# Attention mixers written as planned jobs, pinned in order, with tiles laid out in whole lines

## The chip, the cores and the metric
One core of one Trainium2 chip. The metric is device time in microseconds (us). Three runs of the kernel before gave 1289.66, 1289.69 and 1290.18 us, so the median is 1289.69 us.

## The reference, cut to what matters
Two layers over 512 tokens of width 1024, in float32. Each layer is a mixer and then a gated MLP, each behind an RMSNorm and added to the residual; a last RMSNorm ends it.

```python
def reference(x, ...):
    for layer in range(2):
        h = rmsnorm(x, attn_norm[layer])
        if layer % 2 == 0:   # 8 stick-breaking heads + 8 native-sparse heads, one w_in, one w_out
            x = x + even_mixer(h, ...)
        else:                # 16 forgetting-attention heads, softmax(q k^T * scale + cum_q - cum_k), causal
            x = x + odd_mixer(h, ...)
        x = x + conv_glu_ffn(rmsnorm(x, ffn_norm[layer]), ...)
    return rmsnorm(x, final_norm)
```
A stick-breaking head weighs key s by sigmoid(z) times the product of (1 - sigmoid(z)) over later keys, so it needs a reversed cumulative sum along the keys. A native-sparse head adds three gated branches: 31 compressed blocks, selected blocks and a window. With 512 tokens the selection takes every block and the window every key, so both of those are plain causal softmax.

## The kernel before, in words
The activations are kept transposed: eight tiles of 128 features by 512 tokens. Float32 products are made of three fp32r products: a part is split in a high half (ACT, a cast, line 193) and a low half (DVE, a subtraction, line 194), and high x high, low x high and high x low are added in PSUM. One **step** is these three matmuls for one 128-row slice; a **unit** is the eight steps that give 128 output features (line 197). `vgroup` makes values for 128 tokens at a time, `proj` (line 473) multiplies attention outputs by the output weights and adds to the residual. Weight parts are loaded by SP into two `wraw` buffers and split into two `whi`/`wlo` buffers.

Attention runs in pairs of heads, four stick-breaking pairs (`SbPair`) and eight native-sparse ones in layer 0, eight forgetting ones in layer 1. A pair is: scores S on PE, for query blocks 3, 2 and then 0 and 1; for softmax pairs a masked add with a running maximum on DVE (line 401) and the exponential on ACT (line 403), for stick-breaking pairs three ACT functions, scans on DVE and one more ACT function; for softmax pairs a scaling by the inverse sum on POOL (line 416, four instructions for two query blocks); five groups T of four transposes on PE, each copied to the tile `ph` by ACT (lines 425, 426); and the products V with the values. There is one PSUM bank for T, one for V, two double banks for S, two for the dense steps.

`pipeline` walks over the pairs and lays S of one pair, T of the pair before and V of the pair before that in one sequence, and after each piece takes a number of dense steps from the list `Fill`: 28 steps over a pair in the stick-breaking part and 6 later in layer 0, 22 in layer 1. The instructions of each engine then stand in a fixed order. The part of `proj` that uses the first four output tiles is among the fillers; the part with the last four comes after the last pair.

Small tiles (sums, maxima, gates, tables) lie between the large ones in the same pools, and the value parts are 264 or 272 columns wide, so the large tiles behind them begin at different places in a 256-byte line: counting their sizes, `XH` and `XL` begin 32 bytes into one, the output tiles `OH`, `OL` 192 (layer 0) or 160 bytes (layer 1).

Of the kernel before, what the change touches and what calls it, by code (L numbers as in the profile page):

```python
# [70 lines left out]
def pipeline(pairs, fill, steps):  # L71

    p1 = p2 = None
    for n, h in enumerate(list(pairs) + [None, None]):
        seq = []
        if h is not None:
            seq.append(lambda: (h.S((3,)), h.S((2,))))
        if p2 is not None:
            seq.append(p2.V)
        if p1 is not None:  # L80
            seq.append(lambda: p1.T(0))
        if h is not None:
            seq.append(lambda: h.N(2))
        if p1 is not None:
            seq.append(lambda: p1.T(1))
        if h is not None:
            seq.append(lambda: h.S((0, 1)))
        if p1 is not None:
            seq.append(lambda: p1.T(2))
        if h is not None:  # L90
            seq.append(lambda: h.N(0))
        if p1 is not None:
            seq += [lambda: p1.T(3), lambda: p1.T(4)]
        f = steps(n)
        done = 0
        for m, a in enumerate(seq):
            a()
            want = f * (m + 1) // len(seq)
            fill.step(want - done)
            done = want  # L100
        p2, p1 = p1, h
# [3 lines left out]
def trunk(ctx, tc, A):  # L105
    nc = tc.nc
    pe, act, dve, pool, sp = nc.tensor, nc.scalar, nc.vector, nc.gpsimd, nc.sync
# [49 lines left out]
    maskb = cp.tile([P, 2, 2, P], BF, name="maskb")  # L157
# [5 lines left out]
    def load_consts():  # L163
        for t, n in ((ones, "ones"), (ident, "ident"), (mask32, "mask2"), (mk, "mk"), (conv, "conv")):
            sp.dma_start(t, A[n])
        pool.tensor_copy(maskb, mask32)

    def warm():

        z = cp.tile([P, SEQ], BF, name="zero")  # L170
        pool.memset(z, 0.0)
        ps = pp.tile([P, SEQ], F32, tag="t", bufs=1, name="t")
        for n in range(12):
            mm(ps, z[:, 0:P], z, n == 0, n == 11)


    def weights(src, shape, alloc=None, pieces=1):

        w = wp.tile(shape, F32, tag="wraw", bufs=2, name="wraw")
        if pieces > 1:  # L180
            h = wp.tile(shape, F32R, tag="whi", bufs=2, name="whi")
            l = wp.tile(shape, F32R, tag="wlo", bufs=2, name="wlo")
# [5 lines left out]
        if alloc is not None:  # L188
            h, l = alloc(shape)
        else:  # L190
            h = wp.tile(shape, F32R, tag="whi", bufs=2, name="whi")
            l = wp.tile(shape, F32R, tag="wlo", bufs=2, name="wlo")
        act.copy(h, w)  # L193
        dve.tensor_sub(l, w, h.bitcast(F32))  # L194
        return h, l
# [70 lines left out]
    def finish(fp, src, oh, ol):  # L266
# [20 lines left out]
        def square(m, b, ps):  # L287
# [3 lines left out]
            sq = wp.tile([P, SEQ], F32, tag="sq2", bufs=4, name="sq")  # L291
# [64 lines left out]
    HALF = (slice(0, 64), slice(64, 128))  # L356

    class Pair:

        def __init__(self, ap, q, k, vt, vh, get_o, first, last, bias=None, gate=None, extra=None, done=None):
            self.__dict__.update(locals())
            self.started = False

        def start(self):
            if self.started:
                return
            self.started = True
            self.q, self.k = self.q(), self.k()  # L370
            if self.bias is not None:
                self.bias = self.bias()
            self.e = self.ap.tile([P, 2, 1280], F32, tag="e", bufs=2, name="e")
            self.nm = self.ap.tile([P, 2, NB], F32, tag="nm", bufs=2, name="nm")
            self.dn = self.ap.tile([P, 2, NB], F32, tag="dn", bufs=2, name="dn")

        def scores(self, ii, more):

            self.start()
            ps = s_banks()  # L380
            for i in ii:
                w = P * (i + 1)
                o = EOFF[i] - EOFF[ii[0]]
                t = slice(i * P, i * P + P)
                for hd, r in enumerate(HALF):
                    mm(ps[:, hd, o:o + w], self.q[r, t], self.k[r, 0:w], True, more is None)
                if more is not None:
                    for hd, r in enumerate(HALF):
                        more(ps[:, hd, o:o + w], r, i)
            return ps  # L390

        def S(self, ii):
            ps = self.scores(ii, None)
            for i in reversed(ii):
                w = P * (i + 1)
                o = EOFF[i] - EOFF[ii[0]]
                for hd in range(2):
                    ei = self.e[:, hd, EOFF[i]:EOFF[i] + w]
                    nm, dn = self.nm[:, hd, i:i + 1], self.dn[:, hd, i:i + 1]
                    add = mk[:, 384 - P * i:512] if self.bias is None else self.bias[:, hd, EOFF[i]:EOFF[i] + w]  # L400
                    dve.tensor_tensor_reduce(ei, ps[:, hd, o:o + w], add, scale=-1.0, scalar=3.0e38,  # L401
                                             op0=ALU.add, op1=ALU.min, accum_out=nm)
                    act.activation(ei, ei, AF.Exp, bias=nm, scale=-1.0, accum_out=dn)  # L403
            if self.extra is not None and 0 in ii:
                self.extra.S()

        def N(self, b):

            dn = self.dn[:, :, b:b + 2]
            dve.reciprocal(dn, dn)  # L410
            if self.gate is not None:
                dve.tensor_mul(dn, dn, self.gate[:, :, b:b + 2])
            for i in (b + 1, b):
                for hd in range(2):
                    ei = self.e[:, hd, EOFF[i]:EOFF[i] + P * (i + 1)]
                    pool.tensor_scalar(ei, ei, self.dn[:, hd, i:i + 1], 1.0, op0=ALU.mult, op1=ALU.mult)  # L416

        def T(self, n):
            if n == 0:
                self.ph = self.ap.tile([P, 2560], F32, tag="ph", bufs=1, name="ph")  # L420
            ps = pp.tile([P, SEQ], F32, tag="t", bufs=1, name="t")
            for hd, j in TGRP[n]:
                for i in range(j, NB):
                    o = POFF[hd][j] - 512 * n + (i - j) * P
                    pe.transpose(ps[:, o:o + P], self.e[:, hd, EOFF[i] + j * P:EOFF[i] + j * P + P], ident)  # L425
            act.copy(self.ph[:, 512 * n:512 * n + 512], ps)  # L426
            if self.extra is not None and n == 4:
                self.extra.T()

        def V(self):  # L430
            vt, o = self.vt(), self.get_o()
            for j in (0, 1, 3, 2):
                w = SEQ - j * P
                for hd, r in enumerate(HALF):
                    p0 = POFF[hd][j]
                    mm(o[r, j * P:SEQ], vt[:, self.vh + hd, j], self.ph[:, p0:p0 + w],
                       self.first and j == 0, self.last and j == 2)
            if self.done is not None:
                self.done(o)

    class SbPair(Pair):


        def S(self, ii):
            def more(ps, r, i):
                for n in range(2):
                    mm(ps[:, i * P:i * P + P], maskb[r, 0, n], maskb[r, 1, n], False, n == 1)
            ps = self.scores(ii, more)
            e0 = EOFF[ii[0]]
            w = sum(P * (i + 1) for i in ii)  # L450
            z, e = ps[:, :, 0:w], self.e[:, :, e0:e0 + w]
            lt = self.ap.tile([P, 2, SEQ], F32, tag="lt", bufs=2, name="lt")
            l = lt[:, :, 0:w]
            act.activation(l, z, AF.Abs)  # L454
            act.activation(l, l, AF.Exp, scale=-1.0)
            act.activation(l, l, AF.Ln, bias=1.0)
            dve.scalar_tensor_tensor(l, z, 0.0, l, op0=ALU.max, op1=ALU.add)  # L457
            for i in ii:
                o = EOFF[i] - e0
                for hd in range(2):  # L460
                    ei, li = e[:, hd, o:o + P * (i + 1)], l[:, hd, o:o + P * (i + 1)]
                    dve.tensor_tensor_scan(ei[:, ::-1], li[:, ::-1], li[:, ::-1], 0.0, op0=ALU.add, op1=ALU.bypass)  # L462
            dve.tensor_sub(e, z, e)  # L463
            act.activation(e, e, AF.Exp)
# [578 lines left out]
```

## Time and profile before
| | us |
|---|---|
| median of the runs | 1289.69 |
| the profiled execution, its own time | 1291.93 |
| its span, first to last instruction | 1290.1 |
| PE busy, DVE busy, ACT busy, POOL busy | 1271.2, 693.7, 555.7, 147.9 |
| layer 0: head and first units; attention; last part of the output projection | 0 to 41; 41 to 292; 292 to 313 |
| MLP 0 | 313 to 674 |
| layer 1: norm and first units; attention; last part of the output projection | 674 to 726; 726 to 899; 899 to 921 |
| MLP 1 and the final norm | 921 to 1290 |

Busy time of PE counts a matmul from its start to a modelled end, so two matmuls in a row overlap, and a short wait can hide in it. Where PE's own pace matters, the starts of its instructions are compared.

### The profile page before, as it was taken

Reading aid. Unit: us, or ns where it says so; the run is one execution under the profiler, and the core shown is the slowest. Engines: PE = TensorE matmul, PEld = TensorE weight load, DVE = VectorE, ACT = ScalarE, POOL = GpSimd, SP = SyncE. Lnnn points to the kernel's source line nnn. Section 1 sums busy time; section 2 is a strip of 40 time slices with the busy share of each in tenths; the row PEclk is TensorE's granted clock in tenths of the full one; section 3 lists DMA queues with packets and bytes.
Section 4 is the critical chain, followed back from the end, with each engine's and each line's share of the span. In section 5 each row is a group of like instructions: output and inputs, shape, how many; then the busy total and the mean of one; then the engine's idle time right before and its main releaser. Section 6 shows DMA issues by size and latency. Waiting matters only on the chain.

```text
span 1290.1 us, 16521 instructions
## 1 busy us (share of the span) xinstructions
PE 1271.2 (99%) x6338; PEld 1002.1 (78%) x6338; DVE 693.7 (54%) x1142; ACT 555.7 (43%) x948; POOL 147.9 (11%) x206
## 2 busy tenths in 40 slices
PE   8999999999999999999999999999999999999997
PEld 5876856567888888888888877866788888888886
DVE  7468665538655434565443443344755543556534
ACT  6556465645433223334342554444533322333442
POOL 0000042223000000000111433321200000000010
PEclk9999999999999999999999999999999999999999
DMA  6315201003333233232344453411333223333232
GB/s 224 95 59 147 87 21 42 19 26 123 98 99 94 78 106 107 92 98 89 94 127 141 145 151 92 120 51 51 122 98 98 88 90 100 108 94 94 88 99 90
DMA packets 50639, 124.00 MB, mean 96 GB/s; under 512 B 6320, under 2 KB 15792, under 8 KB 50560
## 3 DMA queue, kind: packets, MB, share of 16 engines
q1 hardware_dynamic: 49040, 121.35, 31.0%
q10 hardware_dynamic: 1520, 1.59, 0.4%
q8 instruction: 50, 0.82, 0.3%
q14 instruction: 29, 0.24, 0.1%
HBM read 119.28 MB, written 2.13 MB: 94 GB/s over the span
## 4 chain that ended last, share of the span: by engine, by line
PE 93%; DVE 3%; ACT 2%; issue 1%; DMA 1%; SPq 0%; DVEq 0%; ACTq 0%
PE mm L115 80%; PE s L115 6%; PE o L115 4%; PE t L425 3%; DVE e L462 1%; DVE wlo L194 0%; ACT whi L193 0%; DMA x<-x 0%; ACT xh L248 0%; DMA wraw<-wu 0%; DVE lt L457 0%; DVE acc L239 0%; ACT lt L454 0%; DVE e L463 0%; DVE e L401 0%
## 5 line engine op out<-in xcount | busy, mean ns | idle before, releaser
L115 PE MATMUL mm<-xh,whi 128*128 128x512 f32 x936 | 372.2, 398 | 0.9 <-ACT xh L248 0.6
L115 PE MATMUL mm<-xh,wlo 128*128 128x512 f32 x936 | 365.1, 390 | 1.6 <-DVE wlo L194 1.6
L115 PE MATMUL mm<-xl,whi 128*128 128x512 f32 x936 | 365.5, 391 | 0.1
L193 ACT CAST whi<-wraw 128x1024 fp32r<-128x1024 f32 (+2 forms) x219 | 200.0, 914 | 383.5 <-PE mm L115 362.7
L194 DVE TENSOR_TENSOR wlo<-wraw,whi 128x1024 fp32r<-128x1024 f32 (+2 forms) x219 | 236.4, 1079 | 137.4 <-ACT whi L193 134.7
L115 PEld LDWEIGHTS mm<-xh,whi 128*128 128x128 f32 x936 | 175.8, 188 | 44.8 <-issue 8.8
L115 PEld LDWEIGHTS mm<-xl,whi 128*128 128x128 f32 x936 | 175.8, 188 | 40.0 <-DVE xl L249 1.8
L115 PEld LDWEIGHTS mm<-xh,wlo 128*128 128x128 f32 x936 | 176.1, 188 | 37.0 <-DVE wlo L194 2.2
L115 PE MATMUL mm<-gh,whi 128*128 128x512 f32 (+2 forms) x352 | 135.0, 383 | 0.0
L115 PE MATMUL mm<-gl,whi 128*128 128x512 f32 (+2 forms) x352 | 134.8, 383 | 0.0
L115 PE MATMUL mm<-gh,wlo 128*128 128x512 f32 (+2 forms) x352 | 134.8, 383 | 0.0
L416 POOL TENSOR_SCALAR e<-e,dn 128x512 f32<-128x512 f32 (+3 forms) x128 | 78.1, 629 | 176.9 <-DVE dn L410 83.9
L403 ACT ACTIVATE e<-e,nm 128x512 f32<-128x512 f32 (+3 forms) x128 | 70.4, 551 | 50.2 <-DVE nm L401 50.2
L426 ACT COPY ph<-t 128x512 f32<-128x512 f32 x100 | 58.1, 581 | 69.6 <-PE t L425 69.4
L783 DVE TENSOR_TENSOR a<-mm,rstd 128x512 f32<-128x512 f32 x44 | 30.4, 691 | 92.1 <-PE mm L115 91.9
L237 POOL COPY acc<-sq 128x512 f32<-128x512 f32 x4 | 2.8, 706 | 651.4 <-ACT sq L234 651.4
L489 DVE TENSOR_TENSOR x<-x,mm 128x512 f32<-128x512 f32 x62 | 42.6, 686 | 64.2 <-PE mm L115 63.9
L115 PEld LDWEIGHTS mm<-gh,wlo 128*128 128x128 f32 x352 | 66.1, 188 | 13.0
L115 PEld LDWEIGHTS mm<-gl,whi 128*128 128x128 f32 x352 | 66.1, 188 | 12.8
L115 PEld LDWEIGHTS mm<-gh,whi 128*128 128x128 f32 x352 | 66.1, 188 | 12.8
L791 DVE TENSOR_TENSOR b<-mm,rstd 128x512 f32<-128x512 f32 x44 | 30.4, 692 | 72.4 <-PE mm L115 72.3
L787 ACT ACTIVATE tt<-tt 128x512 f32<-128x512 f32 x44 | 27.8, 632 | 86.8 <-DVE tt L786 86.8
(167 smaller groups left out, 1644.3 us busy)
## 6 DMA issues: line engine op xcount, KB each, us to landing
wraw<-wfi SPq DMA_DIRECT2D x88, 512.0 KB
wraw<-wu SPq DMA_DIRECT2D x31, 512.0 KB
wraw<-wfo SPq DMA_DIRECT2D x32, 384.0 KB
wraw<-wfo SPq DMA_DIRECT2D x32, 320.0 KB
wraw<-wo SPq DMA_DIRECT2D x32, 256.0 KB
cb<-cd SPq DMA_DIRECT2D x8, 512.0 KB
x<-x SPq DMA_DIRECT2D x14, 256.0 KB
wraw<-wv SPq DMA_DIRECT2D x6, 528.0 KB
```

Source lines behind the costliest of these rows:

```text
L115: pe.matmul(out, l, r, start=st, stop=sp_)
L193: act.copy(h, w)
L194: dve.tensor_sub(l, w, h.bitcast(F32))
L403: act.activation(ei, ei, AF.Exp, bias=nm, scale=-1.0, accum_out=dn)
L416: pool.tensor_scalar(ei, ei, self.dn[:, hd, i:i + 1], 1.0, op0=ALU.mult, op1=ALU.mult)
L425: pe.transpose(ps[:, o:o + P], self.e[:, hd, EOFF[i] + j * P:EOFF[i] + j * P + P], ident)
L426: act.copy(self.ph[:, 512 * n:512 * n + 512], ps)
L462: dve.tensor_tensor_scan(ei[:, ::-1], li[:, ::-1], li[:, ::-1], 0.0, op0=ALU.add, op1=ALU.bypass)
L489: dve.tensor_add(X[m], X[m], ps)
L783: dve.tensor_mul(a, ps, rstd)
L787: silu.append(act.activation(t, t, AF.Silu).ins)
L791: dve.tensor_mul(b, ps, rstd)
```

## The change
Both mixers are no longer walked over by `pipeline`. Every piece becomes a `Job` of one engine with a cost in microseconds, the jobs that it needs, a priority, and tokens for the buffers that it takes and gives back. `Plan.run` is a list scheduler inside the kernel: it goes forward in planned time, picks on each engine the job that can begin first (among those within 0.03 us the one with the smallest priority number), and calls it. While it runs, every instruction of PE, ACT, DVE, POOL and SP is pinned in the order in which it was called. Priorities on PE are V 10, T 20, S 30 and dense steps 100 and up; elsewhere weight loads and splits have 1.2, output copies 1, the work on scores 2. The cost of a job is written out by hand.

Also: `ph` gets two buffers (one before); the first values of layer 0 move from the part ahead of the attention into the plan; the gates' 24 columns, spread before over three value groups (3 x 264), go to the last (256, 256, 280); output projections load two or four tiles' weights as one part, and for output tiles 4 to 7 the two late slices that are ready earlier are multiplied ahead of the last pair (four more adds to the residual on DVE in each layer); rows of `whi` and `wlo` are rounded up to whole multiples of 128 bytes, small tiles go to a pool of their own at the end, `maskb` and `zero` leave the first pool. The rope needs one buffer less. The MLPs and the final norm are unchanged. After it, every tile that a dense matmul reads begins 32 bytes into a line, by the sizes.

```diff
-def pipeline(pairs, fill, steps):
...
+class Plan:
+    LAG = 0.08
...
+    def _when(self, j):
+        t = self.free[j.eng]
+        for d in j.deps:
+            if d.end is None:
+                return None
+            if d.eng != j.eng:
+                t = max(t, d.end + (0.25 if d.eng == "PE" else self.LAG))
+            elif d.lat:
+                t = max(t, d.end + self.LAG)
+        for n in j.take:
+            if not self.bufs[n]:
+                return None
+            t = max(t, min(self.bufs[n]) + self.LAG)
+        return t
+
+    def run(self):
+        while self.jobs:
...
+            for r in ready.values():
+                t0 = min(t for t, _ in r)
+                t, j = min((x for x in r if x[0] <= t0 + self.wait.get(x[1].eng, 0.03)), key=lambda x: x[1].prio)
+                if best is None or t < best[0]:
+                    best = t, j
...
+            self.free[j.eng] = t + j.cost
+            j.end = t + j.cost + j.lat
...
+            j.fn()
...
+    def weight_parts(shape):
+        wide = [P, shape[1], -(-shape[2] // 32) * 32]
+        return [wp.tile(wide, F32R, tag=t, bufs=2, name=t)[:, :, 0:shape[2]] for t in ("whi", "wlo")]
...
+        def weights(self, src, shape, place=None, token="w", split=None):
...
+            a = self.plan.add("SP", 0.35, load, self.prev_load, prio=p, take=("wraw",), lat=3.3)
+            b = self.plan.add("ACT", 0.19 + 0.00085 * n, hi, a, prio=p, take=(token,))
+            c = self.plan.add("DVE", 0.16 + 0.00104 * n, lambda: dve.tensor_sub(...), b, prio=p, give=("wraw",))
...
+        def dense(self, w, k0, n, mv, after=(), end=True):
...
+                j = self.plan.add("PE", 0.69, step, w[1], j, *(after if k == 0 else ()), prio=100 + self.seq, ...)
...
+                j = plan.add("PE", 0.1 + 0.00167 * w2 + (0.1 if sb else 0), S, q[1], k[1], ..., prio=30 + u + 0.001 * len(sj),
+                             take=("s", "e") if ii == (3,) else ("s",), give=give if ii == (0, 1) else ())
...
+                        ex[i, hd] = plan.add("POOL", 0.28 + 0.0008 * P * (i + 1), sc, j, prio=2 + u)
...
+                j = plan.add("PE", 0.42, T, *need, tj[0] if tj else None, prio=20 + u + 0.001 * g,
+                             take=("t", "ph") if g == 0 else ("t",), give=())
+                tj.append(plan.add("ACT", 0.6, lambda g=g: act.copy(...), j, prio=1, give=("t",)))
...
+            j = plan.add("PE", 2.4 + (0.64 if cmp else 0), V, vt[1], self.prev_v, *need, ..., prio=10 + u, ...)
...
-            pipeline(pairs, fl, lambda n: 28 if n < 4 else 6)
-            fl.add(*[proj(m, [(A["wo0"][m][:, 4:8], 4)], OH[4:], OL[4:], lambda m: feed(m, 1)) for m in range(NK)])
+            part([6, 7], 0, 4, (oj[6],))
+            part(range(4, 8), 4, 2, (oj[6],))
+            part([0, 1], 4, 4, (oj[7],), last)
+            part([2, 3], 4, 4, (oj[7],), last)
+            part(range(4, 8), 6, 2, (oj[7],), last)
+            inorder[0] = True
+            plan.run()
```

## Rows read from the trace of the kernel before

**Rows 1.** The page's first part: the span, and for each engine its busy time, share of the span and instructions.
```profile
span 1290.1 us, 16521 instructions
PE 1271.2 (99%) x6338; PEld 1002.1 (78%) x6338; DVE 693.7 (54%) x1142; ACT 555.7 (43%) x948; POOL 147.9 (11%) x206
```

**Rows 2.** Busy time of each engine in stretches: the stretch, its length, then PE, weight loads (PEld), DVE, ACT and POOL, each with its count, then the granted clock, the share of the DMA engines and GB/s.
```profile
41.00:165.00 124.00, 120.35 (x792) 95.71 (x792) 81.81 (x115) 72.06 (x109) 1.61 (x4) 0.99 0.30 91
165.00:292.00 127.00, 125.16 (x670) 75.66 (x668) 70.52 (x226) 73.07 (x192) 38.03 (x66) 1.00 0.09 27
313.30:673.60 360.30, 360.17 (x1587) 297.62 (x1586) 190.37 (x237) 129.59 (x163) 10.35 (x8) 1.00 0.31 97
726.00:884.00 158.00, 158.00 (x935) 120.53 (x934) 65.72 (x171) 77.36 (x186) 54.40 (x80) 1.00 0.37 102
884.00:899.40 15.40, 15.15 (x79) 8.68 (x77) 4.12 (x7) 6.03 (x11) 0.00 (x0) 1.00 0.10 29
920.80:1267.00 346.20, 346.07 (x1538) 286.70 (x1536) 181.72 (x225) 124.36 (x157) 7.14 (x6) 1.00 0.31 95
```

**Rows 3.** The chain that ended last, in order of time: start, length, engine, tile, line and count. The first two are dense stretches, the last part of layer 0's output projection with the start of the MLP, and the MLP; then a scores block, a run of two dense steps and a V block of layer 1.
```profile
292.05 21.42 PE mm L115 x92
320.60 348.46 PE mm L115 x1536
...
746.36 1.70 PE s L115 x8
748.06 1.58 PE mm L115 x6
749.64 2.30 PE o L115 x16
```

**Rows 4.** PE's instructions in order of time at six places in layer 0 and, last, at one in layer 1 where a run of dense steps begins behind a scores block: start, length, line, operation, out<-in, shapes, count, and in brackets the idle time before and what ended it.
```profile
82.73 0.50 PE L115 MATMUL mm<-xh,whi 128*128 128x512 f32 x1
83.63 0.50 PE L115 MATMUL mm<-xh,wlo 128*128 128x512 f32 x1 [0.40 <-DVE wlo L194]
...
92.45 0.39 PE L115 MATMUL mm<-xl,whi 128*128 128x512 f32 x1
94.05 0.66 PE L425 MATMUL t<-ident,e 128*128 128x128 f32 x4 [1.21 <-ACT ph L426]
...
125.37 0.87 PE L115 MATMUL s<-k,q 64*128 64x384 f32 x4
128.28 0.85 PE L115 MATMUL mm<-wc,gt 128*62 128x64 f32 x10 [2.04 <-DVE wlo L194]
...
252.88 0.66 PE L425 MATMUL t<-ident,e 128*128 128x128 f32 x4
253.82 0.71 PE L115 MATMUL s<-k,q 64*128 64x128 f32 x6 [0.29 <-DVE nm L401]
...
286.15 2.37 PE L115 MATMUL o<-ph,vt 128*64 128x512 f32 x14
289.19 0.50 PE L115 MATMUL mm<-o,whi 128*128 128x512 f32 x1 [0.68 <-ACT o L470]
...
290.22 0.63 PE L115 MATMUL mm<-o,whi 128*128 128x512 f32 x2
291.49 0.46 PE L115 MATMUL mm<-o,whi 128*128 128x512 f32 x1 [0.63 <-DVE x L489]
292.05 0.50 PE L115 MATMUL mm<-o,wlo 128*128 128x512 f32 x1
...
747.99 0.50 PE L115 MATMUL mm<-xh,whi 128*128 128x512 f32 x1
748.33 0.40 PE L115 MATMUL mm<-xh,wlo 128*128 128x512 f32 x1
```

**Rows 5.** Groups of instructions by line, engine, operation and shape, over the whole run: count, then busy time in us, mean ns of one, and idle time before them with what ended it. The splits of a whole part on ACT and DVE and the copy of a transposed group on ACT.
```profile
L194 DVE TENSOR_TENSOR wlo<-wraw,whi 128x1024 fp32r<-128x1024 f32 x122 | 151.1, 1239 | 53.5 <-ACT whi L193 53.4
...
L193 ACT CAST whi<-wraw 128x1024 fp32r<-128x1024 f32 x122 | 128.4, 1052 | 216.1 <-PE mm L115 198.5 <-DMA wraw<-wu 11.8 <-PE s L115 4.0
L426 ACT COPY ph<-t 128x512 f32<-128x512 f32 x100 | 58.1, 581 | 69.6 <-PE t L425 69.4
```

**Rows 6.** The same view for POOL's scalings, and for PE's weight loads of T and V.
```profile
L416 POOL TENSOR_SCALAR e<-e,dn 128x512 f32<-128x512 f32 x32 | 23.9, 759 | 102.9 <-DVE dn L410 30.4 <-DVE dn L412 24.4 <-ACT oh L470 21.8
L416 POOL TENSOR_SCALAR e<-e,dn 128x384 f32<-128x384 f32 x32 | 21.9, 696 | 0.0
L416 POOL TENSOR_SCALAR e<-e,dn 128x128 f32<-128x128 f32 x32 | 17.0, 542 | 0.0
L416 POOL TENSOR_SCALAR e<-e,dn 128x256 f32<-128x256 f32 x32 | 16.1, 517 | 74.0 <-DVE dn L410 53.5 <-ACT ph L426 18.5 <-DVE dn L412 2.0
...
L425 PEld LDWEIGHTS t<-ident,e 128*128 128x128 f32 x400 | 46.2, 140 | 24.2 <-ACT ph L426 9.2 <-issue 4.8 <-POOL e L416 2.7
L115 PEld LDWEIGHTS o<-ph,vt 128*64 128x64 f32 x320 | 21.6, 136 | 24.2 <-issue 23.0 <-ACT ph L426 0.5 <-DVE nm L401 0.2
```

**Rows 7.** Instructions in order of time in layer 1: four scalings on POOL in one pair, the DVE split that ran beside them, and the same four scalings in the next pair.
```profile
762.90 2.59 POOL L416 TENSOR_SCALAR e<-e,dn 128x256 f32<-128x256 f32 x4 [5.33 <-DVE dn L410]
...
763.57 1.34 DVE L194 TENSOR_TENSOR wlo<-wraw,whi 128x1024 fp32r<-128x1024 f32 x1 [0.76 <-ACT whi L193]
...
786.03 1.63 POOL L416 TENSOR_SCALAR e<-e,dn 128x256 f32<-128x256 f32 x4 [8.96 <-DVE dn L410]
```

More of the change, by code (lines that the diff above doesn't have):

```diff
@@ L68, in get, with __init__, __getattr__, call @@
         return d[key]
-def pipeline(pairs, fill, steps):
[L73 to L101, printed above, removed]
+class Ordered:
+    def __init__(self, tc, engine, on, dma=False):
+        self.tc, self.engine, self.on, self.dma = tc, engine, on, dma
+    def __getattr__(self, name):
+        f = getattr(self.engine, name)
+        if name.startswith("preload") or (name.startswith("dma") and not self.dma):
+            return f
+        def call(*a, **k):
+            r = f(*a, **k)
+            if self.on[0]:
+                self.tc.keep_in_program_order(r)
+            return r
+        return call
@@ L187, in weights @@
         sp.dma_start(w, src)
[L188 to L192, printed above, removed]
         act.copy(h, w)
@@ L356, in trunk @@
     HALF = (slice(0, 64), slice(64, 128))
[L358 to L387, printed above, removed]
-                    for hd, r in enumerate(HALF):
[L389 to L464, printed above, removed]
-        def N(self, b):
-            pass
@@ L543, in k_use, with v_use @@
                 return use
-            def v_use(key, j):
+            def v_use(key):
                 def use(tb, ps):
@@ new lines, in values, with out, gate_rows @@
+            def values(key, g, n, places=((v_own, "vw"), (None, "w")), more=None):
+                tag = "vn" if key == "n" else "vt" + "AB"[key]
+                def out(tb):
+                    if tb == 0:
+                        VT[key] = ap.tile([P, 4, NB, 64], F32, tag=tag, bufs=1, name="vt")
+                    return VT[key]
+                a = A[f"wv0_{g}"]
+                return M.values([a[0], a[1]], n, places, out, more)
+            def gate_rows(tb, b, j):
+                return plan.add("ACT", 0.26, lambda: act.activation(gates[:, tb], b["ps"][:, 256:280], AF.Exp, scale=nrt[:, tb:tb + 1]),
+                                j, prio=1, give=("mm",))
@@ new lines, in layer0 @@
+            for p in range(4):
+                oj[p] = M.pair(p, *SB[p], (lambda p=p: VT[p // 2], v1 if p > 1 else v0), 2 * (p % 2), lambda p=p: o_tiles(p),
+                               sb=True, give=("q", "k"))
+            part = lambda ms, a, n, after, use=None: M.project(A["wo0"], ms, a, n, OH, OL, after, use)
+            for kind, p in order:
+                if kind == "q":
+                    nq[p] = NQ(p)
+                else:
+                    part([p, p + 1], 0, 4, (oj[3], lx))
@@ new lines, in layer0 @@
+            for p in range(4):
+                c = dict(p=p, bd=ck, vz=cvz, cm=cm, cv=cv, gate=gate, gj=gj)
+                o = {}
+                for b, key in ((1, ks), (2, kw)):
+                    oj[4 + p] = M.pair(4 + 2 * p + b - 1, nq[p], key, (lambda: VT["n"], vn), 2 * (b - 1), (lambda p=p: o_tiles(4 + p)) if b == 2 else None,
+                                       gate=gate[:, b, 2 * p:2 * p + 2], gj=gj, cmp=c if b == 1 else None, o=o, first=False, last=b == 2,
+                                       give=("q",) if b == 2 else ())
@@ new lines, in layer1 @@
+            part = lambda ms, a, n, after, use=None: M.project(A["wo1"], ms, a, n, OH, OL, after, use)
+            oj = {}
+            for p in range(NK):
+                oj[p] = M.pair(p, *R[p], (lambda p=p: VT[p // 2], vj[p // 2]), 2 * (p % 2), lambda p=p: o_tiles(p), bias=gates(p),
+                               give=("q", "k"))
+                if p % 2:
+                    plan.add("SP", 0.0, lambda: None, M.prev_v, prio=0, give=("vt",))
+            for m in range(0, NK, 2):
+                part([m, m + 1], 0, 4, (oj[3],))
@@ L941, in trunk @@
+            part(range(4, 8), 4, 2, (oj[5],))
+            last = lambda m, j: M.feed(m, 3, j)
+            part([0, 1], 4, 4, (oj[7],), last)
+            part([2, 3], 4, 4, (oj[7],), last)
+            part(range(4, 8), 6, 2, (oj[7],), last)
+            inorder[0] = True
+            plan.run()
+            inorder[0] = False
     layer1()
```

671 lines of the change are left out of this document (481 added, 190 removed).

## The prediction, made before the change was run
> **What bounds the kernel now.** The page's first part comes first: PE is busy 99% of the span, DVE 54% and ACT 43% [rows 1]. By itself that says little, since a matmul's end is modelled. So the stretches come next [rows 2]: the reader is to see that PE has no idle time at all over the main part of layer 1's attention (158.00 us of 158.00), almost none in the MLPs, and 3.65 + 1.84 us in layer 0's attention; and that no other engine is full there (DVE 66% at most). Then the chain, for PE's own pace [rows 3]: in the MLP 1536 matmuls of 512 columns take 348.46 us, 226.9 ns each; in the last part of layer 0's output projection 92 take 21.42 us, 232.8 ns each. Last the order of time on PE around its waits, by starts [rows 4]. The kernel is bound by PE's work. What an order of jobs can give back is the time in which PE waits, not the work.
>
> **What the change removes: PE's waits.** Neighbouring starts in layer 0, less what the same neighbours need when nothing is late [rows 4]. A first matmul after a scores block: 0.90 us, where layer 1 shows 0.34, so 0.56. Last step before a transpose: 1.60 less 0.23 is 1.37. Scores before the compression products: the 2.04 that stand in brackets. Transposes before a block of scores: the 0.29 in brackets. V (14 matmuls, 3.03 us) less the 2.30 of a whole block [rows 3]: 0.73. The first projection step behind the last pair: 1.27 less 0.46, and 0.56 less 0.23, together 1.14. The sum is 6.1 us. Each has a cause that an order with more filler can cover: a weight split that comes late, a copy, an ACT output copy after the last pair. Layer 1 has no idle time to give back before 884 us, and 0.25 us after [rows 2]; I count nothing there. So the removal is worth 6.1 us if nothing takes the place of these waits, and zero if the new order only moves them.
>
> **What it adds: new waits from a tight order.** The list scheduler puts V, T and S ahead of dense steps as soon as its costs say that they can begin. Once pinned, PE stands still when such a job is late, with ready dense steps behind it. So I hold the written costs against the rows. A dense step costs 0.69; three matmuls at 226.9 ns are 0.681 [rows 3]. V is 2.4 against 2.30, S for blocks 3 and 2 is 1.70 against 1.70 [rows 3]. A part of 1024 columns costs 1.06 on ACT and 1.22 on DVE, against 1.052 and 1.239; the copy of T 0.6 against 0.581 [rows 5]. These agree within 4%, so most jobs come on time. One doesn't: POOL's scalings. The plan gives 0.69, 0.587, 0.485 and 0.382 us for 512 to 128 columns; times 32 each that is 68.6 us, where the rows show 23.9 + 21.9 + 16.1 + 17.0 = 78.9 [rows 6]. The 10.3 us too few come in lumps: four scalings took 1.63 us in one pair and 2.59 in the pair before, where a DVE split of 1.34 us ran beside them [rows 7]; the plan has 1.73 for the four. The transposes wait for the scalings. In the old order PE's loads for T waited on POOL 2.7 us in all [rows 6], because filler lay between. In the new one the loss lies between 0 (each lump falls in slack) and 10.3 (each lands on PE; more if the new order puts splits and scalings together more often). I take 2.2, nearest to the 2.7 that reached PE before, since the other costs in that chain are not short. Queued behind a late T on PE are dense steps; behind these, their evacuations and the next weight buffer; none of it feeds back into POOL.
>
> The Trainium skill speaks against the change here ("SBUF — State Buffer", section "Who interferes with whom"): a DVE instruction with two SBUF inputs shuts out a GpSimd instruction that reads SBUF, for its whole length. The lump just shown agrees with it. By the rule alone the lumps recur wherever a split meets a scaling, which the plan does not model; the sum by rule would carry up to the price of the second rival below.
>
> **What it moves.** The first values of layer 0 go behind the start of the plan, so stick-breaking pairs start some 6 us earlier; PE is full on either side of that point, so it is worth nothing by itself. The value columns stay 792, the same matmul work. Four more adds per layer on DVE, about 0.69 us each by their cost in the plan, lie in stretches where DVE is busy 66% or less [rows 2]; uncovered they would be 5.5 us together, but each is behind a matmul group that PE is already past. Weight loads in larger parts carry the same bytes, at a DMA share of 9 to 37% in these stretches [rows 2]. The second `ph` buffer lets T begin while V of the pair before still reads; PE had work then. The sequencing of SP matters for ropes, whose small loads wait for an evacuation with weight loads queued behind; two weight buffers ahead are two units, about 11 us, which covers it. A block of scores or V between dense steps breaks PE's pace: the two steps between them took 1.58 us instead of 6 x 0.2269 = 1.36, so 0.22 per switch [rows 3]. The plan has the three S blocks apart where a bank is late (one switch more in each of 20 pairs, +4.4) or blocks side by side (as many fewer, -4.4); I take 0 and keep both ends. The `zero` and `mask32` tiles now share two buffers with the squares of the start; 0 to 1.2 us (two first squares), taken as 0.
>
> **The lines.** The steps of the output projection read `OH` and `OL`, 160 or 192 bytes into a line, at 232.8 ns, and the MLP's read tiles at 32 bytes at 226.9 [rows 3]. That two things differ is not proof that one makes the other. If it is the place in the line, all 2 x 64 steps x 3 = 384 matmuls gain 5.9 ns, 2.3 us; if it is what else runs there, nothing. I take 2.0, since both stretches are plain dense ones with DVE and ACT at work.
>
> **The sum.** -6.1 + 2.2 - 2.0 = -5.9 us. Against the profiled execution's 1291.93 (1.8 more than its span) that is 1286.0; that execution stands 2.2 above the median, so against the median of 1289.69 it is 1283.8 us.
>
> **The rivals.**
> *The waits move, and nothing is gained.* The 6.1 us come back at other places and the lines do nothing: 1289.7, within 2.6 us. For it: layer 1 is already without idle time under the old order, so its fixed sequence was not bad. Against: layer 0's waits have single late causes, and the plan has at all times unblocked dense work until the last pair.
> *Slower.* In each of the 16 softmax pairs the first transpose waits out a split beside the scalings. At 1.24 us [rows 5] that is 19.8, and with the gains kept (6.1 + 2.0) the time is 1301.4. It decides from about 7 of 16 pairs on (8.1 / 1.24). For it: the rows of the lumps [rows 7] and a cost that is short. Against: the four undisturbed scalings, 1.63, are shorter than their cost of 1.73, so a slack comes with each pair.
> *More.* The waits all go, the lines give 2.3, and attention blocks put side by side save two switches in each of 20 pairs: 6.1 + 2.3 + 8.8 = 17.2, so 1272.5. For it: V, T and S have the lowest numbers, so they follow each other when ready. Against: one bank for T and one for V force dense work between.
> *Weight loads show headroom.* Their share is 77%, 60% and 76% in the three attention stretches and 82.6% in the MLP [rows 2]. If an order could bring the first three to 82.6%, (95.71 + 75.66 + 120.53) / 0.826 = 353.4 us would do for 409, and the time would be 1234. Against: V holds PE 2.30 us per block [rows 3], and its 20 blocks hold 21.6 us of loads [rows 6], 1.08 each, with PE never waiting; the share is low by shape. The Trainium skill ("Perfetto Trace Analysis", section "Identifying the Most-Contended Engine") has load share as the measure of PE's headroom; by that rule this rival would be the forecast, and the rows for V disagree.
>
> **How the numbers follow.** My forecast (waits mostly gone, 1278 to 1287) has 0.54, no gain 0.16, slower 0.15, more 0.13, headroom 0.02. The first, fourth and fifth are faster by over 0.2% (2.6 us, about what a measurement of this kernel can tell from no change): 0.69. Same 0.16, slower 0.15. The range of 1273 to 1293 leaves out most of the slower case's upper part and the far ends of the faster ones.
>
> **What would show it.** In the changed profile: PE's busy time about equal, the span shorter by the missing pauses; no bracket over 0.5 us on PE in 41 to 292 us; output projection matmuls at 227 ns a start; scalings still in lumps, with T behind them late at a few places. It is wrong if layer 1's attention, which has no idle time now, changes by more than 2 us, if PE's starts show waits for POOL or DVE in most pairs, or if the projection stays at 232.8 ns.

## The result and the profile after

The changed kernel takes 1283.15 us (median, 1281.73 to 1284.14) against 1289.93 for the one before beside it; the ratio is 0.9946, 95% interval 0.9929 to 0.9963. The profiled execution took 1281.73 us.

The page's first part, which answers to [rows 1]:

```profile
span 1279.6 us, 16397 instructions
PE 1257.2 (98%) x6338; PEld 999.1 (78%) x6338; DVE 699.0 (55%) x1134; ACT 553.9 (43%) x924; POOL 140.2 (11%) x206
```

PE does the same 6338 instructions in 14.0 us less busy time, while the span is 10.5 us shorter. So PE is idle for longer than before. The stretches tell where. These run from one layer's first statistics matmul to that of its MLP, so each holds one attention from end to end, layer 0's first, then layer 1's; columns as in [rows 2]. Of the kernel before:

```profile
22.10:313.30 291.20, 285.63 (x1655) 204.83 (x1656) 184.56 (x380) 166.55 (x334) 50.36 (x77) 0.99 0.24 71
673.60:920.80 247.20, 246.73 (x1395) 189.29 (x1395) 111.99 (x252) 116.49 (x264) 77.82 (x104) 1.00 0.38 112
```

Of the changed kernel:

```profile
22.30:303.10 280.80, 272.71 (x1655) 201.18 (x1655) 187.97 (x376) 164.81 (x318) 47.69 (x77) 1.00 0.24 73
663.50:910.20 246.70, 245.10 (x1395) 189.14 (x1393) 112.62 (x248) 116.89 (x256) 72.49 (x104) 1.00 0.36 111
```

In layer 0 the same 1655 instructions hold PE 12.9 us less, and its idle time grows from 5.57 to 8.09 us. Layer 1 moves by 0.5 us, and the MLP's 1536 matmuls take 348.43 us, as in [rows 3]. The whole gain is in layer 0's attention, and it is in work, not in waits. (The two profiled executions differ by 10.2 us, the medians by 6.8: the one of before stood 2.0 above its median, the one of after 1.4 below.)

About 1.6 of the 12.9 us are the clock's and not the order's. In this execution of the kernel before, the granted clock was at half (1.2 instead of 2.4 GHz) from 128.8 to 132.2 us, behind a wait of 2.04 us; the first line is that stretch, the second the work in it:

```profile
128.80:132.18 3.38, 3.38 (x29) 3.16 (x27) 3.36 (x8) 0.20 (x1) 0.52 (x1) 0.50 0.03 5
```

```profile
128.28 3.19 PE L115 MATMUL mm<-wc,gt 128*62 128x64 f32 x32 [2.04 <-DVE wlo L194]
```

These 32 matmuls took 3.19 us here and 2.00 in the first experiment below, whose layer 0 has the full clock; from their start to that of the third dense matmul behind them 4.05 us go by, against 2.49. The changed kernel's profiled execution has the full clock in all of layer 0.

Which work: the chain of the kernel before over 8 us of layer 0's last eight pairs (start, length, engine, tile, line, count; a count of 2 is one head's one float32 matmul, which the profile shows as two instructions):

```profile
169.16 1.00 PE o L115 x2
170.16 1.06 PE s L115 x4
171.22 0.59 PE t L425 x4
171.81 0.85 PE s L115 x4
172.66 0.59 PE t L425 x4
173.24 1.00 PE o L115 x3
174.24 0.43 PE mm L115
174.67 1.44 PE o L115 x9
```

and blocks of the changed kernel in the same part:

```profile
194.82 2.30 PE o L83 x16
...
225.81 1.06 PE s L83 x4
226.87 2.30 PE o L83 x16
```

A scores product of 512 columns for both heads takes 1.06 us (x4); one head's of V alone takes 1.00 (x2). The two heads use different halves of PE and run together when they are neighbours in the order. In the old order scores and transposes stood between V's first matmul and its partner, and a dense matmul behind it, and the block cost 1.00 + 1.00 + 1.44 = 3.44 us (the chain lists 14 of its 16 instructions), where a whole block takes 2.30. By starts, layer 0's V blocks took 33.8 us before and 27.4 after, its scores 41.1 and 35.0: 12.5 us together. Sorted in this way, where a wait counts with the instruction before it, transposes took 2.2 us more, and value products 2.9 more. The Trainium skill ("TensorE: Matmul & The Clock Gate", section "The mechanism" of Part 3) says that matmuls on different parts of the array overlap, but start and end strictly in program order. The rows agree: what stands between two partners keeps the second from starting beside the first.

PE's waits in the changed kernel (order of time, with the idle time before and what ended it):

```profile
133.33 0.40 PE L83 MATMUL mm<-vhi,xh 128*128 128x280 f32 x1 [0.73 <-ACT gates L83]
...
241.78 0.66 PE L83 MATMUL t<-ident,e 128*128 128x128 f32 x4 [0.68 <-ACT ph L83]
244.78 0.66 PE L83 MATMUL t<-ident,e 128*128 128x128 f32 x4 [0.91 <-ACT ph L83]
248.44 0.73 PE L83 MATMUL o<-pc,vz 128*128 128x512 f32 x2 [0.54 <-DVE pc L83]
272.36 0.63 PE L83 MATMUL t<-ident,cs 128*64 128x128 f32 x4 [0.99 <-ACT ph L83]
274.43 0.73 PE L83 MATMUL o<-pc,vz 128*128 128x512 f32 x2 [1.44 <-DVE pc L83]
...
303.12 1.13 PE L83 MATMUL s<-acc,ones 128*128 128x512 f32 x2 [0.41 <-POOL acc L83]
```

The waits of [rows 4] are gone, and others stand mostly at the last pairs, where the dense steps that may start have run out.

### The profile page after: what moved, and what is told of

Its sections match the earlier page's. It is cut to its first block, busy times and chain, and to the rows that moved or that the text cites. A ratio compares the mean times of both kernels' runs of the same rounds, so it can differ in the third digit from the quotient of the medians.

```text
span 1279.6 us, 16397 instructions
## 1 busy us (share of the span) xinstructions
PE 1257.2 (98%) x6338; PEld 999.1 (78%) x6338; DVE 699.0 (55%) x1134; ACT 553.9 (43%) x924; POOL 140.2 (11%) x206
## 4 chain that ended last, share of the span: by engine, by line
PE 92%; DVE 3%; ACT 2%; DMA 1%; issue 1%; SPq 1%; POOL 1%; DVEq 0%; POOLq 0%; ACTq 0%
PE mm L83 78%; PE s L83 6%; PE t L83 4%; PE o L83 4%; SPq L83 1%; DMA x<-x 1%; DVE x L83 1%; ACT whi L83 1%; DVE xl L83 0%; ACT xh L83 0%; DVE wlo L83 0%; POOL acc L83 0%; DVE acc L83 0%; ACT lt L83 0%; DVE e L83 0%
## 5 line engine op out<-in xcount | busy, mean ns | idle before, releaser
L83 DVE TENSOR_TENSOR wlo<-wraw,whi 128x1024 fp32r<-128x1024 f32 (+2 forms) x207 | 231.5, 1118 | 152.6 <-ACT whi L83 150.1
L83 DVE TENSOR_TENSOR x<-x,mm 128x512 f32<-128x512 f32 (+2 forms) x74 | 49.6, 672 | 76.8 <-PE mm L83 76.7
L83 POOL TENSOR_SCALAR e<-e,dn 128x128 f32<-128x128 f32 (+3 forms) x128 | 70.0, 566 | 162.4 <-DVE dn L83 105.7
L83 ACT ACTIVATE e<-e,nm 128x128 f32<-128x128 f32 (+3 forms) x128 | 70.8, 556 | 30.9 <-DVE nm L83 30.8
L83 PEld LDWEIGHTS mm<-gl,whi 128*128 128x128 f32 x352 | 66.1, 188 | 12.9
L83 PEld LDWEIGHTS mm<-gh,wlo 128*128 128x128 f32 x352 | 66.2, 188 | 12.8
L83 PEld LDWEIGHTS mm<-gh,whi 128*128 128x128 f32 x352 | 66.1, 188 | 12.8
L83 DVE SCALAR_TENSOR_TENSOR tt<-a,conv,tt 128x510 f32<-128x510 f32 x88 | 65.8, 748 | 1.7
```

The source lines that it names most:

```text
L83: r = f(*a, **k)
```

## The experiments

**V's heads in the kernel before.**

```
-                for hd, r in enumerate(HALF):
+                for hd, r in reversed(list(enumerate(HALF))):
                     p0 = POFF[hd][j]
```

> The kernel before, with one edit: in a V block, the matmuls of head 1 are written ahead of those of head 0. Head 1's columns of ph are copied last, so when its first matmul may start its partner may too, and in the program as built none of the 24 V blocks of both layers has another engine job's matmul between partners (5 of 512 columns and 3 of 384 had in layer 0). Theory 'partners' (the two heads' matmuls run at the same time in PE's two row halves, but only as direct neighbours in the instruction order; the change made them neighbours everywhere): V's time in layer 0 falls from 33.8 to 27 to 28 us, S's stays near 41, and the kernel takes 1283 to 1285 against 1289.9. Theory 'waits' (my prediction's first term: what layer 0 could give back is PE's waiting for late parts and copies): no wait loses its cause, so 1289.9 within 1, or slower where V now starts later.

Measured: 1283.8 us, ratio 0.9953 (0.9938 to 0.9968). (There are 20 V blocks, not 24.) V in layer 0 took 27.8 us by starts, scores 42.9. The stretch and one block:

```profile
22.20:306.90 284.70, 277.79 (x1655) 201.49 (x1656) 184.94 (x380) 166.30 (x334) 50.81 (x77) 1.00 0.24 73
```

```profile
201.35 2.30 PE o L115 x16
```

Writing one loop backwards takes 7.8 us of PE's busy time out of layer 0 (1.6 of them the clock's, as above) and 5.9 us off the kernel, while PE's idle time there grows from 5.57 to 6.91 us. Theory "partners" holds; "waits" expected nothing.

**V's heads apart in the changed kernel.**

```
-                for jb in (0, 1, 3, 2):
-                    w = SEQ - jb * P
-                    for hd, r in enumerate(HALF):
+                heads = list(enumerate(HALF))
+                blocks = (0, 1, 3, 2)
+                for jb, (hd, r) in ([(jb, h) for h in heads for jb in blocks] if bias else [(jb, h) for jb in blocks for h in heads]):
+                        w = SEQ - jb * P
```

> The changed kernel, but in layer 1's 8 V blocks head 0's four matmuls come first and then head 1's four, so that partners are no longer neighbours; nothing else in the program differs. Theory 'partners': a block of 1280 columns a head goes from 2.30 us to 4.3 to 4.9 (one head's 512 columns alone took 1.00 us in the kernel before), so 16 to 21 us in all, 1299 to 1304. Theory 'waits': PE's work is the same, 1283 within 1.

Measured: 1295.91 us, 12.8 more than the changed kernel. V's blocks in the chain, here and in the changed kernel:

```profile
730.72 3.86 PE o L83 x15
...
744.12 3.86 PE o L83 x15
```

```profile
729.30 2.31 PE o L83 x16
...
741.17 2.31 PE o L83 x16
```

1.55 us a block, 12.4 for eight. The price of partners apart is thus measured by itself. I had it at 2.0 to 2.6, from 1.00 us for 512 columns; the last matmul of one head still overlaps the first of the other.

**Lines, and then scores, in the kernel before.** Both keep V's loop reversed. The first adds

```
+            if self.ap not in PAD:
+                PAD.append(self.ap)
+                self.ap.tile([P, 32], F32, tag="pad", bufs=1, name="pad")
...
+            c0.tile([P, 56], F32, name="pad0")
```

> The kernel before with V's heads in the reverse order and, besides, two unused pads (128 bytes ahead of lt in the attention pool, 224 ahead of rc in layer 0's c0) so that ph, o6, oh and ol begin 32 bytes into a 256-byte line, where they began at 160 or 192; the order of the instructions is that of the run with V's heads reversed. Theory 'place in a line': 312 of the output projections' 384 matmuls (all but those of o4 and of oh7) go from 231 to 233 ns to 227, 4 to 6 ns each, so 1.2 to 1.9 us off the 1283.8 of that run: 1282. Rival (no effect of these tiles' place): 1283.8 within 0.6.

Measured: 1282.99 us, 0.8 below the run without pads; the ranges touch (1282.11 to 1283.58, 1283.58 to 1284.66). By starts, dense steps in both attentions took 0.9 us less. The sign is as expected, the size under it. It is not settled: in the two profiled executions a wait for a DMA ahead of the compression products differs by as much (2.35 us without the pads, 1.46 with them).

The second adds to that

```
+                with tc.issue_after(LT[0]) if LT and self.gate is not None else ExitStack():
+                    for hd, r in enumerate(HALF):
+                        mm(ps[:, hd, o:o + w], self.q[r, t], self.k[r, 0:w], True, more is None)
...
+                    LT[:] = [pe.transpose(ps[:, o:o + P], self.e[:, hd, EOFF[i] + j * P:EOFF[i] + j * P + P], ident).ins]
```

> As the run with V's heads reversed and the pads, and in layer 0's last eight pairs the scores' matmuls are issued behind every transpose written before them, so that no transpose comes between a scores block's two heads: as built, all V and all S blocks of 256 to 512 columns are whole. Five S blocks were still split in the run with V alone (two of 512 columns, one of 384, two of 256). Theory 'partners': about 2 x 1.05 + 0.8 + 2 x 0.54 = 4.0 us less than the run with the pads, 1278 if S does not now wait for a transpose. Rival (what S costs in layer 0 is waiting, or S now waits for late transposes): 1282 or more.

Measured: 1282.13 us, 0.9 below the run with the pads; 4.0 was expected, and the rival had 1282 or more. The ranges overlap (1281.1 to 1283.47, 1282.11 to 1283.58), so a gain is not shown. The scores fall from 42.0 to 35.2 us, and the stretch shows what happened to that:

```profile
21.80:304.00 282.20, 271.65 (x1655) 199.92 (x1656) 184.75 (x380) 166.32 (x334) 53.77 (x77) 1.00 0.24 73
```

```profile
272.44 0.66 PE L433 MATMUL t<-ident,e 128*128 128x128 f32 x4 [0.50 <-ACT ph L434]
...
275.20 0.63 PE L433 MATMUL t<-ident,e 128*128 128x128 f32 x4 [0.77 <-ACT ph L434]
```

PE's busy time is 271.65 us, less than the changed kernel's 272.71, but 10.55 us are idle. With the work gone, the copies of `ph` end last. The old order with its partners together and two pads is within the spread of the changed kernel (1281.1 to 1283.47 against 1281.73 to 1284.14).

**The changed kernel without pins** (`inorder[0]` stays False).

```
-            inorder[0] = True
+            inorder[0] = False
             plan.run()
```

> The changed kernel with the jobs in the planned order of tracing, but no instruction pinned behind the one before. As built, one scores block of 512 columns has a transpose between its heads again, all V blocks stay whole. Theory 'partners': the neighbours come from the order of the jobs, not from the pins, so V and S keep their gain but for about 1 us; the time is that of the changed kernel within 2 us, 1282 to 1286. My prediction's second term (the pinned order costs 2.2 us in new waits, which filler would cover): 1281. Rival 'the pins are what keeps partners together': V and S rise by most of the 12.5 us that they lost, 1290 or more.

Measured: 1286.0 us, 2.9 more. V stays at 27.4 us and the scores take 37.1, so the order in which jobs are traced, not the pin, keeps partners together. Waits grow:

```profile
22.00:307.20 285.20, 275.65 (x1655) 202.33 (x1655) 185.78 (x376) 163.07 (x318) 48.15 (x77) 0.99 0.23 72
```

PE is idle for 9.55 us instead of 8.09, and busy for 2.9 us more. The granted clock was at 0.50 from 51.3 to 54.7 us in this execution, behind a wait of 1.75 us; value products of 256 columns started every 0.21 us there and every 0.12 before, which makes some 1.5 us (an estimate: 16 starts). Another execution, at a mean granted clock of 0.999, took 1286.03 us all the same, so the clock alone does not make the 2.9. My second term had the sign the wrong way round.

**The place in a line.** First XH and XL are moved alone, to 128 and to 0 bytes into a 256-byte line, then together with the weight parts. The edit for 0 (for 128 it is the tile `ng` that goes, not `rtok`):

```
     XL = [xp.tile([P, SEQ], F32R, name=f"xl{c}") for c in range(NK)]
+    rtok = xp.tile([P, NB], F32, name="rtok")
...
-    rtok = cp.tile([P, NB], F32, name="rtok")
```

> The changed kernel with XH and XL 128 bytes into a 256-byte line instead of 32 (the gain tile stands behind them instead of ahead, all other tiles keep their place in a line). 2880 matmuls of 512 columns of the projections and of the MLPs' first halves read them as moving data. Theory 'place in a line' (my third term): 226.9 ns a start goes up to 230 to 233, so 9 to 17 us more, 1292 to 1300. Rival (what differs is what else runs beside the matmuls): 226.9 as before, 1283 within 1.

> The changed kernel with XH and XL at the start of a 256-byte line (the 32-byte rtok tile stands behind them instead of ahead; all else keeps its place). At 32 bytes their matmuls took 226.9 ns a start, at 128 bytes 230.2 to 237.9. Theory 'place in a line': at 0 no longer than at 32; if it goes on in proportion, some 2 ns less, 2880 x 2 = 5.8 us, 1277 to 1283. Rival (32 is already as good as 0): 1283 within 1.

The third allocates `rtok` behind `wlo`, after layer 0's first `weights`:

```
+            rtok = wp.tile([P, NB], F32, tag="rtok", bufs=1, name="rtok")
```

> As the run with XH and XL at 0, but all tiles from XH to wlo begin at the start of a 256-byte line (rtok behind wlo), the weight parts whi and wlo that stand in PE beside XH among them; gh, gl, oh, ol and the o tiles stay at 32. With X alone at 0 its matmuls took 233.3 ns and those of gh 226.8. Theory 'same place as the weight parts' (a matmul is quick where the moving tile begins at the same place in a line as the weight tile loaded beside it): XH back at 227, gh and oh up to 231 to 233; 1440 x 4 to 6.5 ns is 6 to 9 us over the changed kernel, 1289 to 1293. Theory 'place of the moving tile alone' (32 is a good place, 0 is not): XH 233, gh 227, 1297.7 again. Theory 'each tile off 32 costs': XH over 233 and gh over 229, 1303 or more.

Mean ns between starts of neighbouring 512-column matmuls in layer 0's MLP, 310 to 660 us, from the starts of the order of time:

```
kernel                     xh, xl at  weights at  gh, gl at  ns, xh and xl   ns, gh and gl   us
changed                    32         32          32         226.5 to 227.0  226.3 to 226.9  1283.15
after_x_at_128             128        32          32         230.2 to 237.9  226.4 to 227.1  1298.13
after_x_at_0               0          32          32         233.2 to 233.5  226.5 to 227.1  1297.74
after_x_and_weights_at_0   0          0           32         226.5 to 227.0  233.3 to 233.5  1290.31
```

The order of time shows it in starts. With X alone at 0, three matmuls take 0.70 us:

```profile
400.13 0.40 PE L83 MATMUL mm<-xh,whi 128*128 128x512 f32 x1
...
400.83 0.40 PE L83 MATMUL mm<-xh,whi 128*128 128x512 f32 x1
```

With X and weights at 0, X takes 0.68 and gh 0.70:

```profile
400.13 0.39 PE L83 MATMUL mm<-xh,whi 128*128 128x512 f32 x1
...
400.81 0.39 PE L83 MATMUL mm<-xh,whi 128*128 128x512 f32 x1
```

```profile
640.35 0.40 PE L83 MATMUL mm<-gh,whi 128*128 128x512 f32 x1
...
641.05 0.39 PE L83 MATMUL mm<-gh,whi 128*128 128x512 f32 x1
```

The first run agreed with my third term; the second refuted it as I had written it, since 0 is as bad as 128. The third decides: 0 is good once the weights are at 0, and 32 is bad then. In these five pairs of places, a matmul keeps its pace where its moving tile begins at the same place in a line as the weight tiles loaded beside it; no third place was tried for both. The Trainium skill ("SBUF — State Buffer", section "Who interferes with whom") gives PE two independent read ports, one for the moving tile and one for weight loads, and says that PE never waits for anyone. It names no cost of a place in a line; these rows show one of 3.5 to 11 ns a matmul, and the measurement decides. Whether it is the two reads that meet was not tried.

**Where dense steps are spent.**

```
-            part(range(4, 8), 4, 2, (oj[6],))
+            part(range(4, 8), 4, 2, (oj[5],))
```

> The changed kernel, but layer 0's part of output tiles 4 to 7 over pairs 4 and 5 may start when pair 5 is done (its inputs are ready then), not pair 6. PE waits 0.68, 0.91 and 0.54 us at 241 to 249 us of the changed kernel, where no dense step may start, and 0.99 and 1.44 at 272 to 276, at the last pair. Theory 'waits for want of dense steps, and where these are spent decides': the first three shrink by up to 2.1 us and the last two grow by the same or less, 1281 to 1283.5. My first term (an order with filler takes waits away one by one): 1281.

Measured: 1284.99 us (1283.36 to 1285.39), 1.8 more. The waits at 241 to 249 are gone, those at the last pair have grown:

```profile
268.14 0.65 PE L83 MATMUL t<-ident,e 128*128 128x128 f32 x4 [0.93 <-ACT ph L83]
...
272.65 1.06 PE L83 MATMUL t<-ident,cs 128*64 128x128 f32 x4 [0.68 <-ACT ph L83]
275.16 1.22 PE L83 MATMUL o<-pc,vz 128*128 128x512 f32 x2 [1.44 <-DVE pc L83]
276.31 6.53 PE L83 MATMUL o<-ph,vt 128*64 128x512 f32 x32
```

```profile
270.16:280.40 10.24, 7.45 (x27) 3.62 (x28) 0.69 (x1) 1.75 (x3) 0.00 (x0) 0.50 0.14 47
```

Dense steps spent early are missing late: the waits have moved, and PE's idle time in layer 0 is 8.07 us, as against 8.09. The time that was lost in the profiled execution is the clock's. It was at 0.50 from 270.2 to 280.4 us, behind these waits (last line; columns as in [rows 2]), so that two V blocks took 6.53 us instead of 4.53, and PE's busy time in layer 0 is 3.6 us longer than the changed kernel's. The first theory had the waits right and nothing of the clock; the second expected a gain and missed.

**The tail turned, then the MLP's first units too.** In both layers:

```
+            part(range(4, 8), 6, 2, (oj[7],), last)
             part([0, 1], 4, 4, (oj[7],), last)
             part([2, 3], 4, 4, (oj[7],), last)
-            part(range(4, 8), 6, 2, (oj[7],), last)
```

> The changed kernel, but at the end of both attentions the late part of output tiles 4 to 7 (two steps each) comes ahead of that of tiles 0 to 3 (four steps each); the running sum of squares then starts with tile 4. In the profile of the changed kernel PE waits there for x and for acc, 2.1 us in layer 0 and 2.7 in layer 1 by starts, since a tile's chain (add on DVE, two on ACT, a split on DVE, a sum on POOL, up to 1.44 us on one engine) is longer than two steps (1.38 us) and shorter than four (2.75). Theory 'the last tiles' chain sets the end': 3 to 4.7 us less, 1278.5 to 1280. Rival 'the MLP's first unit waits instead' (for XH of tile 3, and the statistics for the same last sum): 1283 within 1.

Measured: 1282.9 us, no change that can be told. The rival held; the waits went into the MLP's first unit:

```profile
297.24 0.47 PE L83 MATMUL mm<-xh,whi 128*128 128x512 f32 x1 [0.80 <-DVE x L83]
...
300.04 0.50 PE L83 MATMUL mm<-xh,whi 128*128 128x512 f32 x1 [0.51 <-ACT xh L83]
...
302.07 1.12 PE L83 MATMUL s<-acc,ones 128*128 128x512 f32 x2 [0.63 <-POOL acc L83]
```

The next run lets that unit take its inputs in the order in which they come:

```
+                    ks = (4, 5, 6, 7, 0, 1, 2, 3) if c == 0 else range(NK)
+                    return unit(A["wfi"][layer, 2 * c], use_a, ks=ks), unit(A["wfi"][layer, 2 * c + 1], use_b, ks=ks)
```

> As the run with the tail turned, and the first two units of each MLP take their eight inputs in the order 4 to 7, 0 to 3, the order in which the turned tail makes them. With the tail alone turned, PE waited in the first unit: 0.80 us for a bank (x), 0.51 for XH, 0.63 for acc behind layer 0. Theory 'the last tiles' chain': the wait for XH goes, that for acc shrinks, 1 to 2 us a layer, 1279.5 to 1281. Rival (the sums on POOL set this end whatever the order): 1283 within 1.

Measured: 1279.5 us (1279.32 to 1280.6), ratio 0.9913 (0.9899 to 0.9928), faster than both kernels: 3.6 us less than the changed kernel by the medians, 2.2 less between the two profiled executions, which both have a mean granted clock of 0.998. Behind the last pair one wait is left in layer 0:

```profile
297.19 0.47 PE L83 MATMUL mm<-xh,whi 128*128 128x512 f32 x1 [0.84 <-DVE x L83]
```

**The compressed scores' transposes first**, on top of that:

```
-            j = plan.add("PE", 0.45, T, ready, prio=21 + u, take=("t", "pc"), give=("cs",))
+            j = plan.add("PE", 0.45, T, ready, prio=19 + u, take=("t", "pc"), give=("cs",))
```

> As the run with tail and unit turned, and in layer 0 the transposes of the compressed scores (cs) come ahead of the pair's other transposes instead of behind them, so that pc is ready long before V. With these turned PE waited 0.54 and 1.44 us for pc and 0.68, 0.91 and 0.99 us for copies of ph around it (all at the one bank t). Theory 'a wait goes where its cause goes, as long as dense steps are left': the two waits for pc go, 1.5 to 2.5 us less than 1279.5, 1277 to 1278. Rival 'the bank t is full anyway, so the copies of ph are later by what pc was': 1279.5 within 1.

Measured: 1281.38 us, 1.9 slower than without it. The two waits for `pc` ahead of V are gone, but now the bank is held by `pc` and the transposes behind it wait: in layer 0 PE is idle for 7.77 us, where it was 7.65 without the edit. So far the rival is right. The loss is the clock's again: it was at 0.50 from 250.8 to 257.6 us, behind these waits, a whole V block took 3.42 us there, and PE's busy time in layer 0 is 2.3 us longer.

```profile
247.93 0.66 PE L83 MATMUL t<-ident,e 128*128 128x128 f32 x4 [1.39 <-DVE pc L83]
249.27 0.66 PE L83 MATMUL t<-ident,e 128*128 128x128 f32 x4 [0.69 <-ACT ph L83]
...
255.46 3.42 PE L83 MATMUL o<-ph,vt 128*64 128x512 f32 x16
```

```profile
250.78:257.60 6.82, 6.14 (x18) 2.53 (x20) 1.31 (x4) 2.35 (x5) 1.77 (x5) 0.50 0.01 2
```

## Why the prediction was right in its number and wrong in its reasons

The forecast was 1283.8 and the result 1283.15. Its terms do not hold, so that the two lie so close is luck.

**The bound.** "The kernel is bound by PE's work" was right. "What an order of jobs can give back is the time in which PE waits, not the work" is the step that failed. Order gave back some 11 us of work in layer 0 (12.9 less the clock's 1.6) and no waiting. I had read V's and S's price from whole blocks of layer 1 [rows 3] and held it for the price everywhere. One row should have stopped me: the V block of 14 matmuls in [rows 4] holds PE for 2.37 us, as long as a whole block of 16. Its first matmul had been sent ahead alone and had already cost 1.00 us, up to the next start:

```profile
281.83 1.07 PE L115 MATMUL o<-ph,vt 128*64 128x512 f32 x2
282.83 0.66 PE L425 MATMUL t<-ident,e 128*128 128x128 f32 x4
```

I looked only at the 0.73 us behind the block, which is indeed a wait (0.68 in its bracket, for ACT's `o`).

**First term, -6.1.** The waits named did go, but layer 0's idle time rose by 2.5 us: the rival "the waits move" was right about the waits. With less work in the same chains, other causes end last.

**Second term, +2.2.** In this order of jobs pins save 2.9 us. Scalings on POOL do come in lumps, but no bracket among those shown names them except the last sum of squares; transposes wait for the bank and the copies of `ph`.

**Third term, -2.0.** The mechanism was right in that place counts, mis-stated (place relative to the weights, not place by itself) and mis-sized: -0.8. I took the pace from a stretch of 92 matmuls [rows 3] that held waits besides; at the starts, the tiles at 160 or 192 gave 230 to 233 ns and those of `o4`, at 32, already 227.

**What stands in their place.** From the runs on the old kernel: V's partners -5.9, lines -0.8, scores' partners -0.9, together -7.6 to 1282.1. The changed kernel is at 1283.15, so list scheduler, pins, larger loads and the second `ph` buffer, taken together, bring nothing beyond these that can be measured. Of the three sizes only V's is clear of the spread. Why the scores' partners bring at most 0.9 and not 4.0 is seen above: what they free is idle.

**The signs to look for.** "PE's busy time about equal" was wrong by 14 us, and "no bracket over 0.5 us in 41 to 292" by six brackets. Layer 1 within 2 us and projection steps at 227 ns held; in the changed kernel three of them take 0.68 us:

```profile
290.33 0.62 PE L83 MATMUL mm<-o,whi 128*128 128x512 f32 x2
...
291.01 0.62 PE L83 MATMUL mm<-o,whi 128*128 128x512 f32 x2
```

The rival "more" had the side-by-side blocks as saved switches, 8.8 us; the work that whole blocks save is of that order (12.5 us by starts), by another mechanism.

## What to carry to other kernels

Where two matmuls share PE by halves, look in the order of time whether partners are neighbours; a scheduler that sees one ready earlier will send it ahead, and each block then costs half as much again or more, as busy time that no idle column shows. Write first the partner that is ready last. At a tail, order producers and their consumers together: turning one alone moved the wait, turning both gave 2.2 us at the same clock. Before a small difference is put down to an order, compare the granted clock of the stretches: in two runs here the idle time was the same within 0.12 us and the clock made the loss.

## What was not expected of the hardware

The pace of 512-column float32r matmuls depends on where the moving tile begins in a 256-byte line relative to the weight tiles: 226.3 to 227.0 ns at the same place (32 and 32, 0 and 0), 230 to 238 at another (0 or 128 against 32, 32 against 0). Over 2880 matmuls that is 15 us, twice what the change gained. V's float32 products, with `ph` at 160 or at 32 in the kernel before with V's loop reversed, showed nothing of it: layer 1's eight whole blocks took 18.4 us in either.

In layer 0 the granted clock fell to half for 3.4 to 10.2 us behind waits of PE, in some executions and not in others. The changed kernel's profiled execution kept the full clock through its waits of 0.99 and 1.44 us at 272 to 275 us, so these runs do not show when it falls. Its four executions took 1281.73 us at a mean granted clock of 0.998, 1283.01 and 1283.29 at 0.996, and 1284.14 at 0.995. So a wait can cost more than its idle time, by the matmuls that run behind it at half the clock.
